# Attention scores: the low part of the queries kept twice, against the whole stack of keys

## The chip, the core and the metric

The kernel runs on one NeuronCore of a Trainium2 chip. The metric is the device time of one execution in microseconds (us). Three runs of the kernel before took 3002.88, 3005.10 and 3005.45 us; the median is 3005.1 us. The profile is of one further execution of the same program.

Five engines work side by side, each with its own instruction stream: TensorE (PE; the loads of its stationary operands are listed apart as PEld), VectorE (DVE), ScalarE (ACT), GpSimd (POOL) and SyncE (SP), which here issues the DMA transfers. SBUF is the on-chip memory with 128 partitions; PSUM is where TensorE writes its products.

## The reference, cut to what matters

Two layers over 1024 latent tokens (a grid of 16 rows and 64 columns) and 256 context tokens, width 1024. Layer 0 mixes tokens with a Fourier transform and a gated MLP, layer 1 with neighbourhood attention; each layer ends with a convolutional feed-forward net (ConvFFN). The change is in the attention of layer 1, with 16 heads of 64 features:

```python
s_loc = jnp.einsum('bhrqd,bhrikd->bhrqik', qg, kg).astype(jnp.float32) * scale + bias
s_loc = jnp.where(col_mask[:, None, :], s_loc, NEG_INF)
s_ctx = jnp.einsum('bhrqd,bhcd->bhrqc', qg, k_c).astype(jnp.float32) * scale
s = jnp.concatenate([s_loc.reshape(B_, H, rows, GRID_W, n_loc), s_ctx], axis=-1)
p = jax.nn.softmax(s, axis=-1).astype(v.dtype)
o = jnp.einsum('bhrqik,bhrikd->bhrqd', p_loc, vg) + jnp.einsum('bhrqc,bhcd->bhrqd', p_ctx, v_c)
```

Each query sees 8 grid rows by 16 columns of neighbours and all 256 context keys. Everything is float32.

## The kernel before

**Numbers in two parts.** TensorE multiplies operands of the type fp32r, which keeps fewer bits than float32. So an operand x is kept as two parts: `h`, x rounded, and `l = x - h`. A product is the sum of h·h, h·l and l·h; l·l is left out. With only 64 features a head, the parts of a key can be stacked: the tile `k` of a head has the high part of the keys on partitions 0 to 63 and the low part on 64 to 127 (1280 columns: 1024 latent keys, then 256 context keys). The tile `q` has the high part of the queries on both halves. One product of `q` with `k` over 128 rows is thus h·h + h·l; a second one of `ql`, the low part of the queries, with the high part of the keys, over 64 rows, adds l·h in the same PSUM room.

**Blocks.** The tokens of a head are taken in 8 column blocks (`cb`) of 8 grid columns, 128 queries each; two blocks are a pair, and a head has 4 pairs. A block's scores are against its own and its neighbour blocks (3 key tiles of 128, or 2 for the first and the last block, the edges) and the 2 context tiles. So `scores` (lines 1191 to 1210) issues four matmuls a block, in two runs: L1206 (`q`, 128 rows) and L1207 (`ql`, 64 rows) with 384 columns (256 at an edge), then L1206 and L1207 with the context's 256 columns. Every matmul has a stationary operand of its own (the 128 queries of the block in `q` or in `ql`), loaded just before it.

**The stages of a block.** After `scores` (S) come `biasmax` (T, VectorE, L1218: bias and mask added, row minimum of the negated scores), `expo` (E, ScalarE, L1227: the exponential and its sum), `flip` (F, TensorE, L1239: transposes into the PSUM tiles `tl` and `tx`), `high` and `low` (c on ScalarE, L1245, and w on VectorE, L1249: the two parts of the transposed weights), `highx` and `lowx` (X, L1257, and Y, L1261: the same for the context's), `values` (V, TensorE, L1271 to L1278, into `po`), `upper` (L, ScalarE, L1284) and `add` (A, VectorE, L1299). The head's sums are spread by R (`spread`, TensorE, L1316, for every second pair), M (`scale`, ScalarE L1324 and GpSimd L1325) and H (`split`, GpSimd). PSUM holds two tiles `st` for scores, two `tl`, one `tx` and one `po`.

**The order.** On TensorE, VectorE and ScalarE the attention's order is written out by hand (the tuple `order` in `attention`), a pipeline over 64 pairs in which a later stage works on an earlier pair. In one turn TensorE does S of the pair's first block, R, F of both blocks of the pair two turns back, S of the second block, V of the pair three turns back; VectorE does w, T, A, T, w, Y; ScalarE does L, E, c, X, M, c, E. On GpSimd and SyncE a list scheduler sets the order when the program is built. `att_load` (lines 1141 to 1169) loads the operands of a head; it is called for head hd + 1 in the middle of head hd. `k`, `q`, `ql`, `v` and the bias exist once for the even heads and once for the odd ones, so a load of head hd + 2 waits until head hd is done with its tile. The tile `braw`, out of which GpSimd makes a head's bias (L1167), exists once. The loads of head 0 are issued earlier, among those of the products that make queries, keys and values (the qkv stage); those of head 1 wait for the room that this stage gives back.

**After the attention** come the output projection, whose first feature tile is taken while the pipeline drains (L1356), and layer 1's ConvFFN.

Of the kernel before, what the change touches and what calls it, by code (L numbers as in the profile page):

```python
# [15 lines left out]
P = 128  # L16
# [19 lines left out]
def f32(ap):  # L36
    return ap.bitcast(F32)


class Half:  # L40
    """Half of the tokens of a ConvFFN: two column blocks of n operand columns, step apart where they are kept.
    fresh, span, live: (stream, first token, tokens, column) of the tokens that are normed for it, of all of them and
    of those whose neighbours it has; kept: the first of four columns that both halves use."""
# [14 lines left out]
class Squares:  # L58
    """Sums of squares over the feature tiles, by block of tokens, in the room of a ConvFFN's operands."""
# [19 lines left out]
class Ffn:  # L79
    """x += g2 * ConvFFN(norm(x)), one half of the tokens after the other. The first products are taken in blocks,  # L80
    rows (gate, value) and columns (two of tokens) of a pair, inner index in two halves, by the seven products of
    Strassen and Winograd:
      P1 = A00 B00, P2 = A01 B10, P3 = S4 B11, P4 = A11 N4, P5 = S1 T1, P6 = S2 T2, P7 = S3 T3
      S1 = A10 + A11, S2 = S1 - A00, S3 = A00 - A10, S4 = A01 - S2
      T1 = B01 - B00, T2 = B11 - T1, T3 = B11 - B01, N4 = B10 - T2
      C00 = P1 + P2, C01 = P1 + P6 + P5 + P3, C10 = P1 + P6 + P7 + P4, C11 = P1 + P6 + P7 + P5"""
# [5 lines left out]
    # the products in turn, and what is prepared after each for the next tile  # L92
# [4 lines left out]
    # the first two tiles of a half: those products come first that need no sums of blocks of columns  # L97
# [22 lines left out]
    # ---------------------------------------------------------------- operands  # L120
    def part(self, s, op, k, q):
        """Where part q of feature tile k of an operand is kept."""
        i = (self.OPS.index(op) * 4 + k) * 2 + q
        h = self.halves[s]
        lo = i // 14 * h.step
        return self.slabs[i % 14][:, lo:lo + h.n]
# [9 lines left out]
    def begin(self):  # L136
        """The room of the first half's norm and of the next weights."""
        for j, a in enumerate(self.hfa):
            self.hf[j], self.hf[j + 4] = a[:, 0], a[:, 1]
        self.hf[3] = self.t([P, self.w2], "g", bufs=1)  # L140
        self.hf[7] = self.t([P, 8 * P], "wq", bufs=3)[:, :self.w2]
        for names in (("A00", "S2"), ("S1", "S4")):
            t = self.net.t(self.net.wpool, [P, 2, KD, P], "wh", F32R, bufs=2)
            for i, x in enumerate(names):
                self.slots[x] = t[:, :, 4 * i:4 * i + 4]

    def scaled(self, s, i, k, o, r):
        """o: the modulated norm of feature tile k of the i-th stretch of a half's fresh tokens, r being 1 / rms."""
# [11 lines left out]
    def ahead(self):  # L160
        """The norm of the second half, kept in DRAM; a generator, a feature tile of a stretch a step. It takes the
        room of the sums of squares."""
# [17 lines left out]
    def operands(self, s):  # L180
        """The operands of a half out of the norm; a generator, a pair of feature tiles a step."""
# [10 lines left out]
        for j in range(4):  # L192
# [20 lines left out]
            if s == 0:  # L213
                # the room of the others is not free yet, but for half of the first one's
# [9 lines left out]
    # ----------------------------------------------------------------- weights  # L224
    def up_weights(self, f, slots):
        """The steps by which the blocks of the first weights of a pair of gate and value tiles become operand parts
        in slots, in this order (A01, A11 and S3 in any)."""
# [29 lines left out]
    def fetch(self, j):  # L257
        """The j-th part of the second weights on the way: of a pair of feature tiles, for half of the outputs."""
# [14 lines left out]
    # ---------------------------------------------------------------- products  # L273
    def up(self, s, f, hooks, downs, prep, beside):
        """The gated tile f of a half; downs: what the tensor engine does in between; prep: its weights, for later."""
# [109 lines left out]
    def run(self, hooks, beside, early, done):  # L385
        """beside, early: generators of what can be done in the first tiles of the second half and in its last;
        done(d, b) follows the last product of feature tile d and the b-th block of the second half."""
# [41 lines left out]
class Net:  # L429
# [14 lines left out]
    # ---------------------------------------------------------------- helpers  # L444
    def split(self, h, l, src, e=None):
        """src (fp32) = h + l, both rounded to the one-pass matmul format."""
# [8 lines left out]
    def weights(self, src, raw=None, e=None):  # L455
        """A [K, 128] slice of a weight as split operand [128, 2, K/128, 128]."""
# [5 lines left out]
    def proj(self, items, srcs, order=range(KD), by_block=False, hooks=None, apart=False):  # L462
        """items: (w, outs); outs[i] (PSUM, [128, n]) = w^T @ srcs[i]; srcs[i](k, part) is the k-th operand part.
        hooks[i] is called after the i-th step (of the first block)."""
# [24 lines left out]
    # ------------------------------------------------------------------ setup  # L489
    def columns(self, pool, name, parts):  # L490
        """Vectors as columns of 128: parts are (DRAM rows, row, column) of a tile of at most 128 rows of 128."""
# [15 lines left out]
    def setup(self, pool):  # L507
        """What the modulation and the norms need; returns the rest of the setup."""
# [46 lines left out]
    # -------------------------------------------------------------------- ada  # L555
    def ada(self, layer, j, room):
        """Chunk j of the modulation of a layer, for both streams; a generator, one k tile (in a room) a step."""
# [24 lines left out]
    def gains(self, layer, j, streams):  # L582
        """The gains of a norm, where chunk j is its scale."""
# [8 lines left out]
    def ada_sums(self, layer, j, room):  # L592
        """Chunk j for the latents alone, off the tensor engine but for the sums over the partitions; a generator, two
        k tiles of a half a step; what is left is returned."""
# [26 lines left out]
    # ------------------------------------------------------------------- norm  # L621
    def spread(self, col, n):
        """col [128, n]: one value per token, token tile by token tile -> [128, n * 128] PSUM, on all partitions."""
# [7 lines left out]
    def colsum(self, x):  # L631
        """The mean over the features, x [128, tokens] being their partial sums: PSUM [token, token tile]."""
# [6 lines left out]
    def sq_add(self, k, acc, x, tmp):  # L639
        """Feature tile k of a norm: acc += x^2; the last one stays apart in tmp. Returns the sums so far, before it."""  # L640
# [5 lines left out]
    def presum(self, acc):  # L646
        """The share of the mean squares that all feature tiles but the last have: [token, token tile]."""
# [4 lines left out]
    def rstd_col(self, pre, last):  # L652
        """1 / rms of every token, [token, token tile], from pre + the column sums of last."""
# [8 lines left out]
    def roots(self, x):  # L662
        """The scalar engine turns to square roots once x, a column, is there."""
        self.nc.scalar.activation(self.junk, x, AF.Sqrt, bias=self.eps, scale=0.0)

    def spread_to(self, out, col):
        """One value per token, of col, on all partitions of out."""
# [5 lines left out]
    def finish(self, mats, srcs, order, update, ffn, acc, square):  # L673
        """The last two feature tiles mats = (e, w, outs) of a projection, block of tokens by block, and the norm
        that gives a ConvFFN its operands, of which the rest is returned as hooks of its first products."""
# [30 lines left out]
    def norm_block(self, xs, r, hs, layer, n, s, scratch):  # L706
        """Operand parts hs[k] = (H, L) of the modulated norm of a block of tokens xs[k]."""
# [18 lines left out]
    def blocks(self, xl, xc, h):  # L726
        """(columns in [latents | context], stream, feature tiles, operand parts) of the token blocks."""
# [8 lines left out]
    def operand(self, i):  # L736
        """The i-th pair of operand tiles: [context | latents], or the latents alone."""
# [9 lines left out]
    def srcs(self, h, ctx):  # L747
        """Operand getters of the two latent halves and the context."""
# [3 lines left out]
    # ------------------------------------------------------------ even mixer  # L752
    def even(self, h, ada, spill, ws, hooks, close):
        """The head groups of the even mixer, [1024 features, tokens]; returns (latents, context) per group of 128
        features in the order Fourier, gating, and the work left of the last Fourier group, in two steps."""
# [5 lines left out]
        def go(*cols, ws=None, hooks=None, fill=0):  # L761
            """Products for columns of w_in, with the hooks and steps of the modulation in between."""
# [25 lines left out]
        with tc.tile_pool(name="sgu", bufs=1) as pool:  # L788
# [48 lines left out]
            def gate(g):  # L837
                """The normed v of a group as operand parts."""
# [62 lines left out]
    def tables(self, pool):  # L901
        """The tables of the Fourier transforms, as operand parts."""
# [14 lines left out]
    def fourier(self, fl, fc, tables, pool):  # L917
        """f[c, l] (latents, context) becomes the real part of its 2-D transform, y[c', l'], by way of f folded over
        l; a generator of three steps."""
# [70 lines left out]
    # ------------------------------------------------------------- attention  # L990
    def headnorm(self, pk, n, g, pool):
        """pk (PSUM, two heads on the partitions) normed per head and scaled by g: returns the rest of the work,
        which returns it as fp32 in SBUF."""
# [17 lines left out]
    def cols(self, ap):  # L1011
        """A natural block of 8 grid rows [128, 512] seen as [128, column block, row, column]."""
        return ap.rearrange("p (r cb c) -> p cb r c", cb=CB, c=8)

    def percol(self, ap, lo):
        """The same tokens in a tile whose tokens run over (column block, row, column)."""
# [777 lines left out]
```

## Time and profile before

| what | value |
|---|---|
| median of 3 runs | 3005.1 us |
| the profiled execution, first to last instruction (its span) | 3004.0 us |
| instructions | 47545 |
| TensorE busy, share of the span | 95% |
| VectorE, ScalarE, GpSimd busy | 73%, 44%, 42% |
| first and last score matmul start | 1771.1 and 2089.7 us |
| score matmuls L1206 and L1207 | 256 and 256 |

The profile lists no time for the profiled execution other than its span; the span is 1.1 us below the median of the runs. All times within it are counted from its first instruction. Of the views, these are used: the page (busy share of each engine over the span), the windows (busy time of each engine in a stretch, the TensorE clock granted there as a share of full speed, the share of time that the DMA engines work), the chain of waits (the work that ended last, followed backwards; a piece's length is the time from its start to the start of what it released, so on TensorE it is the distance from start to start), the timeline (each instruction with start and duration, and in brackets the idle time of the engine before it), and the list of waits. A form such as "64*128 64x384" of a matmul is rows times columns of the stationary operand, then the moving one. The ends of matmuls are modelled in the trace; their starts are not.

### The profile page before, as it was taken

To read this page: it belongs to the slowest core of one execution; us is meant where nothing else is said; L and a number is where in the kernel's file an instruction comes from. 1 tells how busy PE (TensorE), PEld (TensorE's weight loads), DVE (VectorE), ACT (ScalarE), POOL (GpSimd) and SP (SyncE) were. 2 spreads that over 40 slices of the span, in tenths; PEclk is the share of its full clock that TensorE was granted. 3 is DMA by queue.
4 is the path that set the end of the run, shared out by engine and by line. 5 is a ranking of instruction groups with operands and counts; after the bars stand their busy time and mean duration, and the time that the engine had idled before them with its cause. 6 is when DMAs were issued, how large, how long until landed. Compare 5 with 4: busy or idle time off the path is not lost.

```text
span 3004.0 us, 47545 instructions
## 1 busy us (share of the span) xinstructions
PE 2863.5 (95%) x17978; PEld 2537.8 (84%) x17978; DVE 2203.8 (73%) x3748; ACT 1308.2 (44%) x2448; POOL 1269.4 (42%) x1044
## 2 busy tenths in 40 slices
PE   7999998899999999999999999999979999899998
PEld 4668877899998999998888877777778988799898
DVE  4233578999989999998666657777288777887776
ACT  4312315444444444444433337777254444443443
POOL 0600025455556655553111112333355655666663
PEclk8999999999999999999999979999999999999999
DMA  8763361322223222221333344442223323332233
GB/s 296 217 194 95 114 219 57 108 79 85 82 81 105 78 74 83 78 85 43 115 140 123 109 144 111 114 114 75 64 74 106 94 85 99 105 98 86 85 98 93
DMA packets 334604, 323.45 MB, mean 108 GB/s; under 512 B 15961, under 2 KB 264361, under 8 KB 334377
## 3 DMA queue, kind: packets, MB, share of 16 engines
q1 hardware_dynamic: 330229, 311.49, 34.1%
q0 software_dynamic: 3808, 7.87, 0.9%
q8 instruction: 142, 2.33, 0.3%
q10 hardware_dynamic: 340, 1.06, 0.1%
q14 instruction: 85, 0.70, 0.1%
HBM read 273.66 MB, written 46.71 MB: 107 GB/s over the span
## 4 chain that ended last, share of the span: by engine, by line
PE 69%; DVE 13%; POOL 7%; DMA 5%; issue 4%; ACT 2%; SPq 0%; POOLq 0%; DVEq 0%; ACTq 0%
PE pq L306 20%; PE pq L478 14%; PE pq L376 12%; PE ps L478 6%; DMA wr<-in_ffn_w_up_dram 3%; PE st L1207 3%; PE st L1206 2%; PE pq L566 2%; DVE wh L448 2%; PE tl L1239 1%; POOL ws L241 1%; DVE xl L382 1%; PE ps L487 1%; POOL wh L448 1%; DVE hx L311 1%
## 5 line engine op out<-in xcount | busy, mean ns | idle before, releaser
L376 PE MATMUL pq<-act,wd 128*128 128x320 f32 (+3 forms) x3696 | 637.3, 321 | 55.1 <-DVE xl L382 23.9
L306 PE MATMUL pq<-hs,wh 128*128 128x320 f32 (+3 forms) x4128 | 609.1, 299 | 23.5 <-DVE xl L382 11.5
L376 PEld LDWEIGHTS pq<-act,wd 128*128 128x128 f32 x3696 | 554.7, 192 | 88.2 <-DVE xl L382 27.9
L306 PEld LDWEIGHTS pq<-hs,wh 128*128 128x128 f32 x4128 | 577.4, 191 | 35.0 <-DVE xl L382 15.2
L306 PE MATMUL pq<-hs,wq 128*128 128x320 f32 (+3 forms) x3144 | 469.1, 298 | 7.8 <-DVE wq L448 3.9
L478 PE MATMUL pq<-hs,wh 128*128 128x512 f32 (+3 forms) x2100 | 468.7, 357 | 3.3 <-ACT hs L721 1.7
L306 PEld LDWEIGHTS pq<-hs,wq 128*128 128x128 f32 x3144 | 441.2, 190 | 14.1 <-DVE wq L448 4.9
L478 PEld LDWEIGHTS pq<-hs,wh 128*128 128x128 f32 x2100 | 365.4, 192 | 77.8 <-issue 6.2
L241 POOL TENSOR_TENSOR ws<-wr 128x512 f32<-128x512 f32 x88 | 158.7, 1803 | 402.7 <-DMA wr<-in_ffn_w_up_dram 292.8
L447 ACT ACTIVATE wh<-wr 128x512 fp32r<-128x512 f32 (+1 forms) x223 | 161.7, 725 | 366.5 <-POOL wr L248 205.1
L382 DVE SCALAR_TENSOR_TENSOR xl<-pq,mod,xl 128x320 f32<-128x320 f32 (+5 forms) x616 | 303.7, 513 | 11.9 <-PE pq L376 11.6
L448 DVE TENSOR_TENSOR wh<-wr,wh 128x512 fp32r<-128x512 f32 (+1 forms) x147 | 164.7, 1120 | 197.6 <-ACT wh L447 197.4
L478 PE MATMUL ps<-hs,wh 128*128 128x512 f32 x840 | 244.9, 411 | 5.5 <-ACT hs L721 3.4
L448 POOL TENSOR_TENSOR wq<-wr,wq 128x512 fp32r<-128x512 f32 x152 | 231.1, 1521 | 34.8 <-ACT wq L447 34.7
L311 DVE TENSOR_TENSOR hx<-hx,pq 128x320 f32<-128x320 f32 (+3 forms) x440 | 195.8, 447 | 32.2 <-PE pq L306 24.7
L447 ACT ACTIVATE wq<-wr 128x512 fp32r<-128x512 f32 x262 | 160.1, 623 | 107.1 <-PE pq L306 73.5
L478 PEld LDWEIGHTS ps<-hs,wh 128*128 128x128 f32 x840 | 144.9, 195 | 44.4 <-issue 14.4
L447 ACT ACTIVATE wh<-ws 128x512 fp32r<-128x512 f32 x172 | 107.6, 625 | 169.0 <-PE pq L306 113.5
L251 POOL TENSOR_TENSOR ws<-wr 128x512 f32<-128x512 f32 x88 | 120.5, 1370 | 121.5 <-DVE wh L448 111.2
L1006 DVE RECIPROCAL hsq<-hsq 128x512 f32<-128x512 f32 (+1 forms) x40 | 121.1, 3030 | 53.0 <-ACT hsq L1005 52.1
L999 POOL TENSOR_TENSOR hsp<-hsq,hsp 128x512 fp32r<-128x512 f32 (+1 forms) x40 | 47.1, 1184 | 265.6 <-ACT hsq L998 265.6
L448 DVE TENSOR_TENSOR wd<-wrd,wd 128x512 fp32r<-128x512 f32 x176 | 155.6, 912 | 0.7 <-ACT wd L447 0.7
(310 smaller groups left out, 4584.7 us busy)
## 6 DMA issues: line engine op xcount, KB each, us to landing
wr<-in_ffn_w_up_dram SPq DMA_DIRECT2D x176, 512.0 KB, 4.2
wrd<-in_ffn_w_down_dram SPq DMA_DIRECT2D x88, 512.0 KB, 3.5
adaw<-in_ada_w_dram SPq DMA_DIRECT2D x128, 256.0 KB, 3.5
wd<-in_ada_w_dram SPq DMA_DIRECT2D x32, 512.0 KB, 4.7
wr<-in_odd_w_qkv_dram SPq DMA_DIRECT2D x24, 512.0 KB, 3.8
vd<-kvs SPq DMA_DIRECT2D x8, 1280.0 KB, 7.6
v<-vd SPq DMA_DIRECT2D x16, 640.0 KB, 3.9
kd<-kvs SPq DMA_DIRECT2D x8, 1280.0 KB, 4.6
```

The source lines that it names most:

```text
L241: op(raw["S1"], raw["A10"], raw["A11"], ALU.add)
L251: op(x, raw["A01"], raw["S2"], ALU.subtract)
L306: nc.tensor.matmul(o, w[wn][:, wp, k], self.part(s, bn, k, sp), start=(k == 0 and i == 0), stop=(k == 3 and i == 2))
L311: nc.vector.tensor_tensor(o, x, y, ALU.add)
L376: nc.tensor.matmul(pd, self.wds[j][i][:, wp, d % 4], self.acts[f][:, sp, lo:lo + m], start=(i == 0 and pi == 0), stop=(i == len(fs) - 1 an ...
L382: nc.vector.scalar_tensor_tensor(x, pd[:, a - lo:b - lo], net.mod[:, self.layer, st, 5, d:d + 1], x, ALU.mult, ALU.add)
L447: self.nc.scalar.activation(h, src, AF.Copy)
L448: return (e or self.nc.vector).tensor_tensor(l, src, f32(h), ALU.subtract)
L478: nc.tensor.matmul(o, w(wp, k), s(k, sp), start=(ki == 0 and pi == 0), stop=(ki == len(order) - 1 and pi == 2))
L566: nc.tensor.matmul(acc[32 * q:32 * q + 32, 0:256], self.sT[:, k, :], w[q // 2][:, 256 * (q % 2):256 * (q % 2) + 256], start=(k == 0), stop ...
L1006: nc.vector.reciprocal(r, r)
L1207: nc.tensor.matmul(o, ql[:, c], k[0:HD, kc], start=False, stop=True)
```

## The change

The tile `ql` gets 128 partitions in place of 64, with the low part of the queries on both halves, as `q` has the high part; it is loaded by two transfers in place of one. The second matmul of each run then meets all of `k`, high and low parts, over 128 rows. The result gains the term l·l, which was left out before. The diff also removes comments and docstrings; line numbers stay.

```diff
     def att_load(self, hd):
...
         q = self.t(pool, [P, NL], f"q{e}", F32R)
-        ql = self.t(pool, [HD, NL], f"ql{e}", F32R)
+        ql = self.t(pool, [P, NL], f"ql{e}", F32R)
         v = self.t(pool, [P, 10, 2, HD], f"v{e}", F32R)
         for i in range(2):
             nc.sync.dma_start(f32(k[i * HD:(i + 1) * HD]), self.kd[pr, i, sl])
             nc.sync.dma_start(f32(q[i * HD:(i + 1) * HD]), self.qd[pr, 0, sl])
-        nc.sync.dma_start(f32(ql), self.qd[pr, 1, sl])
+            nc.sync.dma_start(f32(ql[i * HD:(i + 1) * HD]), self.qd[pr, 1, sl])
         nc.sync.dma_start(f32(v).rearrange("p i s c -> p (i s c)"), self.vd[hd])
...
         for lo, kt, n in runs:
             o = s[:, lo:lo + n * P]
             kc = slice(kt * P, (kt + n) * P)
             nc.tensor.matmul(o, q[:, c], k[:, kc], start=True, stop=False)
-            nc.tensor.matmul(o, ql[:, c], k[0:HD, kc], start=False, stop=True)
+            nc.tensor.matmul(o, ql[:, c], k[:, kc], start=False, stop=True)
```

On TensorE, VectorE, ScalarE and GpSimd every instruction keeps its place. On SyncE one transfer is added for each of the 16 heads, and the scheduler places it so. In the attention, for each head, the order on SyncE's queue before (the tiles of head 2; `braw` is the raw bias of the head after it):

```order
L1159 DMA q_2076_16537<-qd 64x1024
L1158 DMA k_2075_16536<-kd 64x1280 x2
L1159 DMA q_2076_16537<-qd 64x1024
L1160 DMA ql_2077_16538<-qd 64x1024
L1152 DMA braw_16763<-bd 128x384
L1161 DMA v_2078_16539<-vd 128x1280
```

and with the change:

```order
L1159 DMA q_2076_16539<-qd 64x1024
L1158 DMA k_2075_16538<-kd 64x1280
L1160 DMA ql_2077_16540<-qd 64x1024
L1158 DMA k_2075_16538<-kd 64x1280
L1159 DMA q_2076_16539<-qd 64x1024
L1160 DMA ql_2077_16540<-qd 64x1024
L1152 DMA braw_16766<-bd 128x384
L1161 DMA v_2078_16541<-vd 128x1280
```

The raw bias and the values stand one transfer of 64 x 1024 numbers (256 KB) further back. The other place is head 0's loads in the qkv stage (`wr` is a weight of that stage, `vd`, `kd` and `qd` are DRAM rooms that the stage writes). Before:

```order
L1159 DMA q_1798_14441<-qd 64x1024 x2
L1160 DMA ql_1799_14442<-qd 64x1024
L1069 DMA vd<-kvs_14151 128x2x1280
L1161 DMA v_1800_14443<-vd 128x1280
L452 DMA wr_14542<-in_odd_w_qkv_dram 128x8x128
L1046 DMA kd<-kvs_13984 128x2x1280
```

and with the change:

```order
L1159 DMA q_1798_14441<-qd 64x1024
L1160 DMA ql_1799_14442<-qd 64x1024
L1159 DMA q_1798_14441<-qd 64x1024
L1160 DMA ql_1799_14442<-qd 64x1024
L1069 DMA vd<-kvs_14151 128x2x1280
L452 DMA wr_14543<-in_odd_w_qkv_dram 128x8x128
L1161 DMA v_1800_14443<-vd 128x1280
L1046 DMA kd<-kvs_13984 128x2x1280
```

Here the load of the next weight has gone ahead of that of the values; behind these rows the stage's order is as before.

## The prediction

> **What bounds the kernel now.** I read the page first, then the windows of the attention, its chain of waits and its timeline.
>
> ```profile
> span 3004.0 us, 47545 instructions
> PE 2863.5 (95%) x17978; PEld 2537.8 (84%) x17978; DVE 2203.8 (73%) x3748; ACT 1308.2 (44%) x2448; POOL 1269.4 (42%) x1044
> ```
>
> TensorE leads over the whole span, but the change touches one stage, so that stage decides. The windows row of its steady part has, in order, the stretch, its length, busy time of PE, PEld, DVE, ACT and POOL, the granted clock, the share of DMA time and GB/s:
>
> ```profile
> 1800.00:2080.00 280.00, 280.00 (x1678) 211.30 (x1677) 201.74 (x485) 204.75 (x483) 89.45 (x144) 1.00 0.45 110
> ```
>
> TensorE is never idle, at full clock; ScalarE is busy 73% and VectorE 72%. So TensorE bounds the stage. What it does with the time stands in the chain of waits (start, length, what), an inner pair with the edge behind it:
>
> ```profile
> 1828.29 0.18 PE st L1206
> 1828.47 0.37 PE st L1207
> 1828.84 0.31 PE st L1206
> 1829.15 0.31 PE st L1207
> 1829.46 0.55 PE po L1271 x3
> 1830.13 0.47 PE po L1277 x4
> ...
> 1831.88 0.48 PE tl L1239 x3
> ...
> 1832.58 0.33 PE tl L1239 x3
> 1832.90 0.22 PE tx L1239 x2
> 1833.24 0.31 PE st L1207
> ...
> 1836.49 0.37 PE st L1316 x2
> ...
> 1849.15 0.55 PE po L1271 x3
> ```
>
> The first and last L1271 rows are four pairs, one head, apart: 19.69 us. Four matmuls of 256 columns in `values` take 0.47 us, 0.118 each; a score matmul of 256 columns takes 0.31 us, one of 384 columns 0.37, but 0.18 where it follows others of 128 rows (1828.29). Whatever comes first after L1207 is longer too: three L1239 take 0.48 us after it and 0.33 elsewhere. The timeline says why:
>
> ```profile
> 1903.48 0.22 PE L1274 MATMUL po<-ph,v 128*128 128x128 f32 x1
> 1903.48 0.13 PEld L1275 LDWEIGHTS po<-ph,v 128*64 128x64 f32 x1
> 1903.54 0.22 PE L1275 MATMUL po<-ph,v 128*64 128x128 f32 x1
> ...
> 1904.24 0.19 PEld L1206 LDWEIGHTS st<-k,q 128*128 128x128 f32 x1
> 1904.35 0.34 PE L1206 MATMUL st<-k,q 128*128 128x384 f32 x1
> ...
> 1904.62 0.18 PEld L1207 LDWEIGHTS st<-k,ql 64*128 64x128 f32 x1 [0.20 <-issue]
> 1904.62 0.44 PE L1207 MATMUL st<-k,ql 64*128 64x384 f32 x1
> ...
> 1904.99 0.19 PEld L1206 LDWEIGHTS st<-k,q 128*128 128x128 f32 x1 [0.19 <-issue]
> 1904.99 0.38 PE L1206 MATMUL st<-k,q 128*128 128x256 f32 x1
> ```
>
> The load at 1904.24 starts 0.11 us ahead of its matmul, under the one before. Those at 1904.62 and 1904.99 sit idle for 0.2 us and start with their own matmul. This happens whenever 64 rows follow 128 or 128 follow 64. A change of columns (128*128 to 128*64, at 1903.54) costs nothing: 0.06 us from start to start. Sharing a PSUM tile isn't the cause, since the four L1277 also add into one. I take the change of rows as the cause: about 0.19 us a time, four times a block.
>
> **The change part by part.** *Score matmuls.* Their number and columns stay. A block in the middle takes 0.18 + 0.37 + 0.31 + 0.31 = 1.17 us now. At prices of unbroken 128-row runs (0.18 for 384 columns, 0.12 for 256) it takes 0.60. That 128 rows stream no slower than 64 shows in the two 0.31 rows, L1206 and L1207 alike. At an edge, L1206 starts where the transposes end, 1832.90 + 0.22 = 1833.12, so the block takes 0.12 + 3 x 0.31 = 1.05; it becomes 0.48. Six blocks and two edges a head: 8 x 0.57 = 4.56 us saved.
>
> *What follows L1207.* Three L1271 take 0.55 and at 0.118 would take 0.35, saving 0.20; three L1239 save 0.48 - 0.33 = 0.15; two L1316 save 0.37 - 0.22 = 0.15. One such exit to V and one to F or R in each of four pairs: 4 x 0.35 = 1.40 us. So TensorE's need of a head falls by 5.96 us, from 19.69 to 13.73.
>
> *Who is late next.* From the windows row ScalarE needs 204.75 / 280 x 19.69 = 14.40 us a head, VectorE 201.74 / 280 x 19.69 = 14.19. Both exceed 13.73, so ScalarE becomes the bound and TensorE keeps about 0.7 us of the gain for itself. What these engines wait for now is almost all TensorE (waiter, releaser, total us, times, longest):
>
> ```profile
> DVE t L1218 <- PE tx L1239: 54.2, 57, 1.2
> ACT low L1284 <- PE po L1278: 39.1, 59, 1.1
> ACT ph L1245 <- PE tl L1239: 21.3, 59, 0.4
> ```
>
> Those waits shrink as TensorE gets ahead. The tightest circle that is left is the single tile `tx`: its transposes, the two copies out of it (X on ScalarE, Y on VectorE), then the next transposes. At 0.33 and 0.22 us for each half F takes 1.1 us, and the copies in the timeline are
>
> ```profile
> 1902.74 0.68 DVE L1261 TENSOR_TENSOR ph<-tx,ph 128x512 fp32r<-128x512 f32 x1
> 1907.08 0.60 ACT L1257 ACTIVATE ph<-tx 128x512 fp32r<-128x512 f32 x1 [0.38 <-PE tx L1239]
> ```
>
> together 2.4 us of a turn of 3.6, so it doesn't bind by itself. Three engines needing 13.7, 14.2 and 14.4 us will not mesh without loss; I take 14.7 us a head, ScalarE's need and 2% (my choice). Its bounds: 13.73, if ScalarE's records overlap so much that TensorE still decides; 16.2, if a third of ScalarE's present idle time (5.29 us) stays. Each of heads 1 to 15 thus gains 4.99 us (5.96 at best, 3.5 at worst): 74.9 (89.4, 52.5).
>
> *Head 0* runs at half clock and beside the loads of head 1:
>
> ```profile
> 1771.09 0.55 PE L1206 MATMUL st<-k,q 128*128 128x256 f32 x1 [1.21 <-issue]
> 1776.42 0.45 SPq L1158 DMA_DIRECT2D k<-kd  x1
> 1794.59 0.41 PE L1206 MATMUL st<-k,q 128*128 128x256 f32 x1
> ```
>
> ```profile
> 1772.00:1776.00 4.00, 4.00 (x9) 2.04 (x8) 1.50 (x4) 1.76 (x3) 0.00 (x0) 0.50 0.88 356
> 1784.00:1788.00 4.00, 4.00 (x10) 2.00 (x8) 2.53 (x7) 2.60 (x6) 0.00 (x0) 0.50 0.99 270
> 1788.00:1792.00 4.00, 4.00 (x15) 3.10 (x15) 1.81 (x4) 1.63 (x4) 1.73 (x2) 0.50 0.07 24
> ```
>
> It takes 23.5 us. The loads of head 1 (2.5 MB with the new one) are issued from 1776.42 on, and those of now (2.3 MB) are through at about 1788, 0.2 MB/us. Keys and queries, 1.7 MB, then take until about 1784.5, so head 0 can shrink by at most 10 us. I take 8, as the switches cost at least as much here; the lower bound is 5, the steady gain.
>
> *The added transfer* costs SyncE one issue of 0.6 us a head and 0.26 MB. Now the loads of a head and of the next raw bias take 9.3 us, from the issue of `q` to the bias operation that waited for them:
>
> ```profile
> 1873.27 0.45 SPq L1159 DMA_DIRECT2D q<-qd  x1
> 1875.68 0.59 SPq L1160 DMA_DIRECT2D ql<-qd  x1
> 1882.58 0.73 POOL L1167 TENSOR_TENSOR bias<-braw,maskr 128x256 f32<-128x256 f32 x1 [2.72 <-DMA braw<-bd]
> ```
>
> With 1.90 MB in place of 1.64 that is 10.8 us, and the tiles are wanted a whole head (14.7 us) after the issue; so it costs nothing, and 16 us for each us beyond that if the cover were gone. Behind the waiting L1167 on GpSimd stand L1337 and L1325, and behind these the next R; L1325 waits for ScalarE anyway:
>
> ```profile
> POOL wr L1325 <- ACT rb L1324: 101.0, 27, 7.7
> ```
>
> 3.7 us each time, so 1.5 us more of waiting ahead of it fits.
>
> Head 0's transfers in the qkv stage cost nothing: TensorE is busy without a break around them (windows row, columns as above), and the stage's next weight now goes ahead of the values.
>
> ```profile
> 1470.00:1510.00 40.00, 40.00 (x203) 33.55 (x202) 30.37 (x25) 15.79 (x28) 7.17 (x6) 1.00 0.63 211
> ```
>
> *Sum.* 74.9 + 8 = 83 us, 3004.0 - 83 = 2921 us of span; the median stands 1.1 us above the span: 2922 us.
>
> **The rivals.**
>
> *TensorE stays the bound* (0.06): 13.73 us a head, 89.4 + 10 = 99 us, 2906 us. For it, TensorE's 100%; against it, ScalarE's 204.75 us.
>
> *Waits stay between the engines* (0.13): the copies of `tx` queue behind E and c on ScalarE, so the next transposes come 0.5 us late in each turn: 14.7 + 4 x 0.5 = 16.7 us a head, 15 x 3 + 5 = 50 us, 2955 us. For it, the order fixed by hand for a turn of 4.9 us; against it, the circle's 2.4 us.
>
> *The loads stay in the open* (0.04): if the cause isn't the change of rows but that these operands can't be loaded under a matmul on the same rows, the scores keep their 0.31 and 0.37 us and the exits theirs: 3004 us of span, 3005 us. For it, the loads at 1904.62 and 1904.99 that wait for their turn; against it, the 0.47 us of four L1277, each with its load, all on 128 rows. [...]
>
> *The clock falls* (0.02), the slower side: TensorE gets idle gaps in each turn, and the gate may answer with half clock as it did from 1772 on. TensorE's need would be up to 27.5 us a head, 16 x 7.8 = 125 us more: 3130 us. It decides from a mean clock of about 13.73 / 19.69 = 0.70. Against it: the array streams the same columns in less time than in the stretch that held 1.00.
>
> **How the numbers follow.** The forecast, ScalarE as the bound with 14.3 to 15.5 us a head, has 0.75: 2922 us, its own range 2910 to 2937. The whole range goes to 2905 below (all bounds at best: 99 us) and to 2948 above (52.5 + 5 = 57.5 us gained), which leaves out the slower and the unchanged case and half of the waiting one. Runs of this kernel tell 0.2% (6 us) from no change. Faster: 0.75 + 0.06 + 0.13 = 0.94; same 0.04; slower 0.02.
>
> **What would show it.** L1206 and L1207 at 0.17 and 0.12 us from start to start in the chain, L1207's loads ahead of their matmuls without the 0.2 us; a head in 14.3 to 15.5 us; ScalarE near 100% of the steady part, TensorE with small gaps ended by ScalarE or VectorE; the chain there passing to ScalarE. Wrong: score matmuls still at 0.31 us (the cause isn't the rows), or scores at 0.12 and a head above 16 us (waits), or waits of L1206 for `ql`'s or `k`'s transfers (loads).

## The result

The changed kernel takes 2920.4 us (median of 4 runs, 2914.1 to 2922.3) against 3005.3 us before; the ratio is 0.9715, with a 95% interval of 0.9701 to 0.9729. That is 2.85% faster, 85 us. 2922 us had been forecast. One slow execution of the kernel before, of 5378 us beside the first experiments, is left out of all ratios.

The page of the profile after, its span, the engines, and the chain's shares by engine:

```profile
span 2919.1 us, 47590 instructions
PE 2772.8 (95%) x17978; PEld 2522.4 (86%) x17978; DVE 2216.9 (76%) x3748; ACT 1302.0 (45%) x2448; POOL 1267.9 (43%) x1044
...
PE 61%; DVE 14%; DMA 7%; POOL 7%; issue 5%; ACT 5%; SPq 0%; POOLq 0%; DVEq 0%; ACTq 0%
```

TensorE's share of the span hasn't moved from 95%, and its busy time fell by 91 us with not one instruction less. "Busy" had held the wait for operands.

The chain of waits, the same part of a turn as shown of before (start, length, what):

```profile
1794.26 0.18 PE st L1206
1794.44 0.18 PE st L1207
1794.62 0.12 PE st L1206
1794.74 0.12 PE st L1207
1794.86 0.33 PE tl L1239 x3
1795.19 0.22 PE tx L1239 x2
...
1796.44 0.35 PE po L1271 x3
```

A middle block takes 0.60 us where it took 1.17, and what follows L1207 has its unbroken price, 0.33 us for three L1239 and 0.35 for three L1271. The timeline has the loads back under the matmul before:

```profile
1863.28 0.28 PE L1206 MATMUL st<-k,q 128*128 128x256 f32 x1
1863.28 0.19 PEld L1207 LDWEIGHTS st<-k,ql 128*128 128x128 f32 x1
...
1863.40 0.29 PE L1207 MATMUL st<-k,ql 128*128 128x256 f32 x1
```

L1207's load starts 0.12 us ahead of its matmul, with no idle time in front. The windows row of the steady part (stretch, length, busy PE, PEld, DVE, ACT, POOL, clock, share of DMA time, GB/s) and two of SyncE's rows, ten heads apart:

```profile
1800.00:1990.00 190.00, 189.31 (x1566) 182.88 (x1565) 185.35 (x452) 185.47 (x449) 87.04 (x140) 1.00 0.77 178
```

```profile
1831.11 0.45 SPq L1159 DMA_DIRECT2D q<-qd  x1
1974.94 0.45 SPq L1159 DMA_DIRECT2D q<-qd  x1
```

A head takes (1974.94 - 1831.11) / 10 = 14.38 us in place of 19.69. VectorE and ScalarE are busy 98% of it, TensorE's records fill 99.6%, and the clock stayed at 1.00. The transfers run at 178 GB/s where they ran at 110.

Where the 85 us came from, within the two profiled executions:

| stretch | before | after | difference |
|---|---|---|---|
| start to first score matmul | 1771.1 | 1771.9 | +0.8 |
| head 0 (first score to head 1's first) | 23.5 | 16.1 | -7.4 |
| heads 1 to 15, at 19.69 and 14.38 each | 295.4 | 215.7 | -79.7 |
| last score to the end | 914.3 | 915.6 | +1.3 |
| span | 3004.0 | 2919.1 | -84.9 |

(The parts are rounded, and the heads are taken at their steady time.) Outside the attention about a microsecond was lost at either end.

### The profile page after: what moved, and what is told of

It reads as the page before. It is cut to its first block, busy times and chain, and to the rows that moved or that the text cites. A ratio compares the mean times of both kernels' runs of the same rounds, so it can differ in the third digit from the quotient of the medians.

```text
span 2919.1 us, 47590 instructions
## 1 busy us (share of the span) xinstructions
PE 2772.8 (95%) x17978; PEld 2522.4 (86%) x17978; DVE 2216.9 (76%) x3748; ACT 1302.0 (45%) x2448; POOL 1267.9 (43%) x1044
## 4 chain that ended last, share of the span: by engine, by line
PE 61%; DVE 14%; DMA 7%; POOL 7%; issue 5%; ACT 5%; SPq 0%; POOLq 0%; DVEq 0%; ACTq 0%
PE pq L306 18%; PE pq L478 15%; PE pq L376 11%; PE ps L478 6%; DMA wr<-in_ffn_w_up_dram 4%; POOL ws L241 2%; DVE xl L382 2%; DVE wh L448 2%; PE pq L566 2%; POOL wh L448 2%; DVE hx L311 2%; PE ps L487 2%; ACT t L1227 1%; POOL wr L248 1%; DMA wd<-in_ada_w_dram 1%
```

## The experiments

The forecast rested on two claims: that the price comes with a *change* between 64 and 128 rows, about 0.19 us each time, and that ScalarE and VectorE take over as the bound just above TensorE's need of 13.73 us. Nine kernels test them. Every head time below is from two rows of SyncE's transfer of the values, ten heads apart, in the way shown above for the queries.

### All scores on 64 rows

```diff
-                nc.tensor.matmul(o, q[:, c], k[:, kc], start=True, stop=False)
+                nc.tensor.matmul(o, q[0:HD, c], k[0:HD, kc], start=True, stop=False)
                 nc.tensor.matmul(o, ql[:, c], k[0:HD, kc], start=False, stop=True)
```

> The kernel before, with both score matmuls on 64 rows: the high part of the queries meets only the high part of the keys (the product of high queries and low keys is left out). Theory (a change between 64 and 128 rows exposes the next operand load, about 0.19 us a time): inside a block no change is left, only one on the way in and one on the way out, 2 instead of 4 a block. TensorE's need is 13.73 + 8 x 2 x 0.19 = 16.8 us a head, 15 x 2.9 + 4 = 48 us saved: about 2957 us (2945 to 2968), score matmuls inside a block at 0.18 and 0.12 us from start to start. Rival 1 (an operand of 64 rows can never be loaded ahead): all four at 0.31 and 0.37 us, a head of 21 us, about 3025 us. Rival 2 (two matmuls that add into the same PSUM room wait for each other): 0.31 and 0.37 us inside the block, no gain, about 3005 us.

Measured: 2952.1 us, ratio 0.9835 (0.9805 to 0.9866) to the kernel before, beside it 3001.5 us; about 49 us faster. Its chain of waits:

```profile
1853.05 0.37 PE st L1206
1853.42 0.18 PE st L1207
1853.59 0.13 PE st L1206
1853.72 0.12 PE st L1207
1853.84 0.48 PE tl L1239 x3
...
1854.54 0.33 PE tl L1239 x3
```

The first score matmul after 128-row work pays (0.37 us for 384 columns), and so does the first work of 128 rows after the block (0.48 in place of 0.33). Between them 64-row matmuls, each with an operand of its own and adding into the same room, run at 0.18 and 0.12 us, just as 128-row ones do. So a 64-row operand can be loaded ahead, and the shared PSUM room costs nothing: both rivals fall. A head takes 16.61 us:

```profile
1819.85 0.33 SPq L1161 DMA_DIRECT2D v<-vd  x1
1985.98 0.33 SPq L1161 DMA_DIRECT2D v<-vd  x1
```

### The same instructions, grouped

```diff
             for lo, kt, n in runs:
                 o = s[:, lo:lo + n * P]
                 kc = slice(kt * P, (kt + n) * P)
                 nc.tensor.matmul(o, q[:, c], k[:, kc], start=True, stop=False)
+            for lo, kt, n in runs:
+                o = s[:, lo:lo + n * P]
+                kc = slice(kt * P, (kt + n) * P)
                 nc.tensor.matmul(o, ql[:, c], k[0:HD, kc], start=False, stop=True)
```

(And `runs` of the last block starts at 256 and 512 in place of 0 and 256.)

> The kernel before, with the four score matmuls of a block in another order: first both of the high queries on 128 rows, then both of the low queries on 64 rows (in the last block of a head the scores lie 256 columns further on, so that its two runs are in two banks). The same instructions, operands and transfers; 2 changes of rows a block instead of 4. Theory: about 2957 us (2945 to 2968), as with all 64. Rival 1 (the price belongs to each 64-row matmul, not to the change): two 64-row matmuls a block as before, no gain, 3005 us. Rival 2 (adding into the same PSUM room): all of the gain, as in the changed kernel, 2920 us.

Measured: 2945.5 us, ratio 0.9815 (0.9781 to 0.9849), 56 us faster. A head takes (1982.18 - 1816.55) / 10 = 16.56 us:

```profile
1816.55 0.33 SPq L1161 DMA_DIRECT2D v<-vd  x1
1982.18 0.33 SPq L1161 DMA_DIRECT2D v<-vd  x1
```

Two thirds of the changed kernel's gain come from writing two lines in another order: same matmuls, same operands, no added transfer. A price per 64-row matmul would have shown no change. The total came out 11.5 us better than the expected 2957: the head time is 0.24 us shorter than the 16.8 expected of two changes a block (3.6 us over 15 heads), head 0 went from 23.50 to 15.37 us and so gained 8.1 us where 4 had been taken, and the kernel before stood at 3001.5 us beside it, not 3005.

### The transfer alone

```diff
-                nc.tensor.matmul(o, ql[:, c], k[:, kc], start=False, stop=True)
+                nc.tensor.matmul(o, ql[0:HD, c], k[0:HD, kc], start=False, stop=True)
```

This and the following diffs are against the changed kernel.

> The changed kernel's 128-partition tile of the low queries and its two transfers a head, but the second score matmul takes 64 rows as before. Theory: the transfer is hidden and the rows are all, so 3005 us (3000 to 3010). Rival (part of the gain comes from the moved loads, or the transfer costs): a change of more than 6 us either way.

Measured: 3003.5 us beside 3001.5, ratio 1.0010 (0.9993 to 1.0026), a head of (2032.50 - 1835.64) / 10 = 19.69 us. The second transfer of the low queries costs nothing that can be told, and the moved loads bring nothing; the whole gain is in the rows.

### Two changes of rows in the changed kernel

```diff
-                nc.tensor.matmul(o, ql[:, c], k[:, kc], start=False, stop=True)
+                r = HD if kt == 8 else P
+                nc.tensor.matmul(o, ql[0:r, c], k[0:r, kc], start=False, stop=True)
```

> The changed kernel with 64 rows only in the low queries' product with the context's keys (the other one keeps 128): 2 changes of rows a block. Theory (price by the change, whatever causes it): about 2957 us (2945 to 2968), the same as the other two kernels with 2 changes. Rival 1 (price by 64-row matmul, about 0.38 us each, of which VectorE and ScalarE hide nothing): half of 85 us given back, 2963 us, but then the grouped order would show no gain. Rival 2 (waits elsewhere set the time): unchanged at 2920 us.

Measured: 2945.1 us, ratio 0.9814 (0.9783 to 0.9846), and a head of (1991.48 - 1825.82) / 10 = 16.57 us. From its chain (L1207 has become L1208):

```profile
1852.70 0.17 PE st L1208
1852.87 0.12 PE st L1206
1852.99 0.31 PE st L1208
1853.30 0.55 PE po L1272 x3
```

```profile
1825.82 0.33 SPq L1161 DMA_DIRECT2D v<-vd  x1
1991.48 0.33 SPq L1161 DMA_DIRECT2D v<-vd  x1
```

The L1208 on 128 rows takes 0.17 us for 384 columns, and the one on 64 rows 0.31 for 256, with 0.20 us more in what follows. Three kernels that have two changes a block by three different ways take 16.61, 16.56 and 16.57 us a head; against 19.69 us with four that is (19.69 - 16.57) / 16 = 0.195 us a change. From there to the 13.74 us that TensorE needs without any (shown below) it is 2.83 / 16 = 0.177, so a change costs 0.18 to 0.20 us. As with the grouped order, the total lies some 12 us under the expected 2957.

### What counts as a change

```diff
-                nc.tensor.matmul(o, ql[:, c], k[:, kc], start=False, stop=True)
+                nc.tensor.matmul(o, ql[0:96, c], k[0:96, kc], start=False, stop=True)
```

> The changed kernel with the low queries' product on 96 rows (they meet the high keys and half of the low keys; half of the added low-by-low term is left out). Theory A (any difference in the number of rows between neighbours exposes the load): four changes a block as in the kernel before, a head of 19.7 us, about 3004 us. Theory B (what counts is whether the array is set to 64 or to 128 rows, and 96 rows are taken as 128): score matmuls at 0.18 and 0.12 us, a head of 14.4 us, about 2918 us.

Measured: 2919.1 us, ratio 0.9717 (0.9685 to 0.9749), a head of (1958.39 - 1814.55) / 10 = 14.38 us: no difference from the changed kernel. The form in the trace is of 96 rows, and the chain is the changed kernel's:

```profile
L1207 PE MATMUL st<-k,ql x256: 277/287/522, 1772.2 to 2003.5; 96*128 96x384 f32 x96, 96*128 96x256 f32 x32
```

```profile
1839.84 0.18 PE st L1206
1840.01 0.18 PE st L1207
1840.19 0.12 PE st L1206
1840.32 0.12 PE st L1207
```

So theory A, that any difference in rows costs, falls. 96 rows beside 128 are free here (14.38 us a head, as with 128 alone) and 64 beside 128 are not (16.57 us a head with two changes a block, 19.69 with four). The times are those of theory B; the reason it gives for them was the author's assumption, which no run shows by itself.

### Who bounds the attention now

Four kernels change the work of ScalarE and VectorE. In the first, `biasmax` and `expo` take 256 columns fewer:

```diff
-            n = s.shape[1]
+            n = s.shape[1] - 256
...
-            nc.vector.tensor_tensor_reduce(out=t[:, :n], in0=s, in1=b[:, bo:bo + n], scale=1.0, scalar=3.0e38,
+            nc.vector.tensor_tensor_reduce(out=t[:, :n], in0=s[:, :n], in1=b[:, bo:bo + n], scale=1.0, scalar=3.0e38,
...
-                src = t[:, keys(cb).index(kt) * P:(keys(cb).index(kt) + 1) * P]
+                at = min(keys(cb).index(kt), t.shape[1] // P - 1)
+                src = t[:, at * P:(at + 1) * P]
```

> The changed kernel, with bias, minimum and exponential on 256 columns less of each block (the scores of two key tiles are left out of the softmax, and the transposes read another tile in their place, so TensorE's work is the same). Takes about 1.7 us a head from ScalarE and 2.1 us from VectorE, leaving 12.3 and 12.0 of 14.38. Theory (ScalarE and VectorE bound the attention, TensorE right behind with a need of 13.73 us a head): a head of 13.8 us, 16 x 0.6 = 9 us faster than the changed kernel, about 2911 us (2906 to 2915). Rival 1 (waits, not the two engines' work): 2920 us. Rival 2 (TensorE's need is well below 13.73): a head of 13.0 or less, 2898 us or less.

The second and third write one line twice:

```diff
             nc.scalar.activation(lo[HD:P], po[HD:P], AF.Copy)
+            nc.scalar.activation(lo[HD:P], po[HD:P], AF.Copy)
```

> The changed kernel with ScalarE's copy of the low half of the output (L1284) issued twice, 4 x 0.40 = 1.6 us a head more for ScalarE alone. Theory (ScalarE has next to nothing left, 14.04 of 14.38 us): a head of about 15.8 us, 16 x 1.4 = 23 us slower than the changed kernel, 2943 us (2936 to 2950). Rival (TensorE still bounds): under 5 us slower, 2920 to 2925 us.

```diff
             nc.vector.tensor_tensor(chunk(of[pr], j)[e * HD:(e + 1) * HD], four(po[0:HD]), four(lo[HD:P]), ALU.add)
+            nc.vector.tensor_tensor(chunk(of[pr], j)[e * HD:(e + 1) * HD], four(po[0:HD]), four(lo[HD:P]), ALU.add)
```

> The changed kernel with VectorE's addition of the two halves (L1299) issued twice, 4 x 0.42 = 1.7 us a head more for VectorE alone. Theory (VectorE is as full as ScalarE, 14.03 of 14.38 us): a head of about 15.8 us, 22 us slower, 2943 us (2936 to 2950). Rival (ScalarE alone bounds, VectorE has room): under 8 us slower.

The fourth is the second's edit on the kernel before.

> The kernel before with the same second copy on ScalarE. Theory (TensorE bounds it, ScalarE is idle 27% of the steady part): no change, 3005 us (3000 to 3010). Rival (ScalarE was on the path before as well): up to 25 us slower, 3030 us.

| kernel | median us | ratio to before, interval | two rows of SyncE, ten heads apart | head us |
|---|---|---|---|---|
| changed | 2920.4 | 0.9715 (0.9701 to 0.9729) | 1831.11, 1974.94 | 14.38 |
| changed, 256 columns fewer | 2906.1 | 0.9667 (0.9649 to 0.9685) | 1813.79, 1951.19 | 13.74 |
| changed, ScalarE + 1.6 us | 2937.8 | 0.9777 (0.9758 to 0.9797) | 1813.53, 1972.95 | 15.94 |
| changed, VectorE + 1.7 us | 2935.3 | 0.9771 (0.9749 to 0.9793) | 1814.27, 1972.12 | 15.79 |
| before, ScalarE + 1.6 us | 3001.3 | 0.9985 (0.9969 to 1.0001) | 1828.25, 2025.12 | 19.69 |

The windows rows of the three kernels behind the changed one, in this order (columns as above):

```profile
1810.00:1970.00 160.00, 159.47 (x1375) 159.06 (x1373) 142.49 (x396) 146.54 (x396) 77.94 (x128) 1.00 0.80 187
```

```profile
1810.00:1970.00 160.00, 153.35 (x1188) 140.92 (x1187) 143.82 (x342) 155.78 (x381) 68.25 (x109) 1.00 0.68 162
```

```profile
1810.00:1970.00 160.00, 154.25 (x1200) 142.45 (x1199) 156.11 (x386) 144.59 (x344) 68.24 (x110) 1.00 0.69 162
```

With less for both, their busy share falls to 89% (VectorE) and 92% (ScalarE), the head stops at 13.74 us, and the lines that head the chain from 1800 to 1990 us are TensorE's alone:

```profile
by line: PE tl L1240 16.8%; PE st L1206 15.2%; PE st L1207 15.2%; PE po L1278 12.7%; PE tx L1240 12.2%; PE po L1272 9.5%; PE st L1317 3.3%; PE po L1279 3.3%; PE po L1275 3.2%; PE po L1276 2.5%; issue 1.0%; POOL bias L1167 0.8%; POOL hs L133
```

So 13.74 us is TensorE's need, and the forecast's 13.73 is confirmed by a kernel in which it decides. With 1.6 us more for ScalarE alone the head grows by 1.56 us, and with 1.7 more for VectorE alone by 1.41; in the kernel before, the same extra work on ScalarE costs nothing. So in the changed kernel each of the two has next to no slack, and TensorE stands 0.6 us behind them. Both added copies also lie on the way of the one tile `po` from TensorE through ScalarE and VectorE back to TensorE, so a longer way could have cost the same. The rows speak for the work itself: the engine that got more is busy 97% and 98%, the other falls to 90%. No kernel put the added work elsewhere. The totals moved by 17 and 15 us where 23 and 22 were expected, the second (2935.3 us) to just below its expected range of 2936 to 2950; the stretch from the first to the last score matmul grew by 22.2 and 20.5 us, from 231.6 (1771.9 to 2003.5) to

```profile
L1207 PE MATMUL st<-k,ql x256: 276/283/522, 1769.6 to 2023.2; 128*128 128x384 f32 x96, 128*128 128x256 f32 x32
```

(1769.4, its first L1206, to 2023.2) and likewise 1769.5 to 2021.6, so the effect in the stage is near the expected one and the rest lies outside it: in these two executions the first score starts 2.5 and 2.4 us sooner, and from the last score to the end takes 1.3 and 2.5 us less.

No kernel here beats the changed one with the whole computation in it. What is left in this stage with TensorE's work as it is comes to at most 14.38 - 13.74 = 0.64 us a head, 10 us, and needs both ScalarE and VectorE relieved; that wasn't tried.

## Why the prediction was right

**The cause** was right, and it was the claim on which all hung. The rows at 1904.62 and 1904.99 of before, loads that wait 0.2 us and start with their matmul, were read as the price of a change of rows; the kernels with two changes show that. It was put as a change of rows; one between 96 and 128 costs nothing, so not every change counts.

**TensorE's need of 13.73 us** was worked out from the prices of unbroken runs elsewhere in the same stage, and 13.74 was measured where it decides.

**Who is late next** was right: ScalarE and VectorE. The size of the term was off. ScalarE's need was put at 14.40 us, from its busy share of before, and 2% was added for waits: 14.7. Measured: 14.38, and ScalarE's records fill 185.47 / 190 x 14.38 = 14.04 us of it. The records of neighbouring instructions overlap when they run back to back (after, ScalarE's L1245 at 1860.00 has 0.49 us and the next one starts at 1860.38) and not when a wait lies between (before, the same at 1881.61, and the next one starts at 1882.27), so the busy time of an engine that waits reads a little too long as its need. The 2% was about right on top of 14.04 (2.4%). That makes 0.32 us x 15 = 5 us more gain than forecast. Against it stand 0.6 us less in head 0 and 2.1 us lost at the two ends, so the total is nearer than its largest term. That the two engines waited before for almost nothing but TensorE was read too simply: VectorE also waited 24.1 us for ScalarE between 1800 and 2090 (L1299 for L1284), a wait that is down to 0.7 us in the list after.

**Head 0** gained 7.4 us for a forecast of 8, and that it came so near is partly luck. The 8 was reasoned from what the changes of rows cost there. What most likely ended head 0 were the loads of head 1, which the forecast had as a limit, with keys and queries there by about 1784.5:

```profile
1782.02 0.52 PE L1239 MATMUL tl<-ident,t 128*128 128x128 f32 x3 [2.46 <-DVE ph L1249]
1782.08 0.59 SPq L1159 DMA_DIRECT2D q<-qd  x1
1787.98 0.36 PE L1206 MATMUL st<-k,q 128*128 128x256 f32 x1 [0.95 <-DVE wr L1299]
1789.17 0.36 PE L1207 MATMUL st<-k,ql 128*128 128x256 f32 x1 [0.84 <-DMA ql<-qd]
```

The row at 1787.98 is head 1's first score. The profile puts its wait down to VectorE, but in all six kernels that have the added transfer and the short head 0 this score starts 5.84 to 5.90 us after the issue of the second transfer of `q` (here at 1782.08), whatever that kernel gives ScalarE and VectorE to do. So the load fits as the end of the wait, and head 0 takes 16.0 to 16.1 us in each of them. Ahead of it TensorE stood still for 2.46 us and the clock came up (0.95 from 1776 to 1780 us; 0.50 in the kernel before); neither was in the forecast. The added transfer itself was waited for once, the 0.84 us in head 1.

**The added transfer** was costed at nothing, and the kernel with the transfer alone says so for heads of 19.69 us. In the changed kernel's shorter heads no engine's wait for `ql` is in the list of waits from 1792 to 1996, so the 0.84 us above are all that shows. GpSimd's waits for the raw bias grew (75.5 us in the stretch from 1792 to 1996, one of them 23.7 us at its start, from 34.4 us between 1800 and 2090 before), but the list of waits of that stretch has nobody who waits for GpSimd:

```profile
POOL bias L1167 <- DMA braw<-bd: 75.5, 11, 23.7
```

**The rivals.** TensorE alone as the bound would have given 2906 us; it is what the kernel with 256 columns fewer shows (2906.1), so it was near, held off by 0.6 us a head. Waits between the engines of 0.5 us a turn did not come. The loads in the open fell: 128-row loads go ahead under 128-row matmuls (L1207's at 1863.28 starts with the L1206 before it and 0.12 us ahead of its own matmul). The clock stayed at 1.00 in the steady part (1800 to 1990 us); that idle gaps of TensorE would bring it down was the author's estimate, and no run tests it by itself.

**The chain** was expected to pass to ScalarE. It does so in part: in the stretch from 1800 to 1990 the lines that head it are

```profile
by line: ACT t L1227 17.6%; PE st L1206 11.5%; PE tl L1239 11.2%; PE st L1207 9.7%; PE po L1277 8.2%; PE tx L1239 7.6%; PE po L1271 6.1%; ACT ph L1245 5.5%; issue 4.9%; ACT ph L1257 4.6%; ACT low L1284 4.0%; PE po L1278 2.1%; ACT rb L1324 2
```

Before, the lines that head it around the attention were all TensorE's. The expected small idle gaps of TensorE hardly show in its busy time (189.31 of 190), because they go into the records of matmuls: L1206, the first of a block, which has the waits, has longer records than L1207 with the same columns (groups of the same stretch: columns, count, busy time, mean ns):

```profile
L1206 PE MATMUL st<-k,q 128*128 128x384 f32 x79 | 32.5, 411 | 0.0
...
L1207 PE MATMUL st<-k,ql 128*128 128x384 f32 x79 | 26.6, 337 | 0.0
```

## What to carry to other kernels

Look at the distance from start to start of matmuls with the same number of columns, not at TensorE's busy share: where it differs, look whether the operand loads start with their matmul. If a matmul on 64 rows stands between ones on 128, pad it (96 and 128 rows both worked here; nothing between 64 and 96 was tried), or at least group the 64-row ones. The transfer that the padding added cost nothing that could be told here (3003.5 us beside 3001.5), the grouping not one instruction, and each change saved was worth 0.18 to 0.20 us of TensorE at a clock of 1.00. Then ask who is second: here 95 us of TensorE's time were freed and 85 came through, since ScalarE and VectorE were nearly as full.

## What was not expected of the hardware

- A 96-row matmul costs no change beside 128-row ones (0.18 and 0.12 us from start to start, 14.38 us a head), while a 64-row one costs about 0.19 us on the way in (0.37 in place of 0.18 us for 384 columns, 0.31 in place of 0.12 for 256) and 0.15 to 0.20 us on the way out (0.48 in place of 0.33 us for three L1239, 0.55 in place of 0.35 for three L1271).
- The clock of TensorE stood at 0.50 in every window from 1769 to 1796 us in the kernel before, although its records fill that time from 1772 on. After the change it is up at 1776 (0.95 to 1780) and drops twice again, to 0.50 from 1784 to 1786 us, behind the wait of 2.46 us that ended at 1782.02, and to 0.50 from 1791 to 1793, behind the waits at 1787.98 and 1789.17:

```profile
1772.00:1776.00 4.00, 4.00 (x14) 3.81 (x15) 3.21 (x8) 3.38 (x6) 0.00 (x0) 0.50 0.66 266
1776.00:1780.00 4.00, 3.56 (x24) 3.22 (x23) 2.00 (x6) 1.04 (x4) 0.00 (x0) 0.95 1.03 384
1784.00:1788.00 4.00, 3.05 (x18) 2.88 (x16) 3.17 (x8) 2.92 (x7) 0.00 (x0) 0.67 1.03 210
1788.00:1792.00 4.00, 3.16 (x17) 2.99 (x18) 1.17 (x3) 1.35 (x4) 0.00 (x0) 0.76 1.07 305
```

The changes of rows come to mind first. But the steady part of the kernel before kept full clock (1.00 from 1800 to 2080 us) with as many changes a block, and two kernels with two changes a block differ: the grouped one is at full clock from 1784 on (first row), the one with all scores on 64 rows still near half from 1792 to 1796 (second row), with first scores at 1772.4 and 1771.3:

```profile
1784.00:1788.00 4.00, 4.00 (x30) 3.30 (x28) 3.71 (x9) 3.58 (x10) 0.00 (x0) 1.00 1.00 221
1792.00:1796.00 4.00, 4.00 (x18) 3.45 (x16) 1.91 (x5) 1.76 (x5) 0.00 (x0) 0.52 0.95 193
```

So the number of changes alone doesn't tell how long the low clock lasts, and what does wasn't tested.
